# A 90 degree rotation of a matrix: hardware loops on three engines, one queue for loads and stores, all outputs gathered by row tile in pairs

## The chip, the core and the metric

## The reference

```python
def setup_inputs():
    return {
        "x": np.random.randn(8192, 8192).astype(np.float32),
        "k": 1,
    }

def reference(x: np.ndarray, k: int) -> np.ndarray:
    return np.rot90(x, k)
```

With k = 1, `out[i, j] = x[j, 8191 - i]`: a transpose whose rows then stand in reverse order. Nothing is calculated. 268 MB are read and 268 MB are written.

## The kernel before

The matrix is cut into 16 macro tiles of 1024 rows (R) and 4096 columns (W). A macro tile is loaded as T = 8 slabs of 128 rows, each slab one DMA of 2 MB (128 partitions with 16 KB each), and gives J = 8 outputs, each 512 rows of the result by 1024 columns, also one DMA of 2 MB. So there are 128 loads and 128 stores. A slab holds one block of 128 rows by 512 columns (CH) for each of the eight outputs; an output needs that block of all eight slabs, 32 squares of 128 x 128.

On-chip, a macro tile lies in a grid of 8 x 8 blocks. One macro tile lies in it by slab and output, the next one the other way round (`kk % 2`), so that a slab of the next macro tile can be placed where an output of this one has just been read. Five blocks of the grid (CORNER) lie in PSUM instead, and the places of four of these in SBUF (STAGES) serve as staging space.

Four engines work as a pipeline:

- SP (line 141) issues the loads into three landing buffers at the start and two of them later on. A load waits until the slab that last lay in its buffer has been placed (`s_copy`).
- VectorE does two things. `place` (line 156) copies a landed slab into the grid: one copy of 4096 columns, or two where part of the slab belongs in PSUM. `to_stage` (line 166) gathers half of the work of 128 x 1024 that PE takes at a time into a staging block, 512 columns, and reverses the columns within it. For each output VectorE makes eight such gathers, then places one slab of the next macro tile, `place(n - 1 + T)`. For the first output of a macro tile (`first`) the last slab is gathered straight from its landing buffer and placed after that.
- PE (line 223) transposes a staging block as four squares into one of three PSUM banks, in a hardware loop of 12 blocks.
- ACT (line 260) copies each bank, 512 columns, into an output buffer. After eight of them it drains, waits for itself (`s_act`) and issues the store (line 267) on its own DMA queue. Three output buffers take turns; for the last eight outputs five buffers do, the two landing buffers among them. For an output's first use of a buffer, ACT waits for the store that last read it (`s_store`).

The first output of a macro tile is gathered by row tile: one block of the grid gives one staging block, and ACT's copy writes four strips of 128 columns, one for each of the four row groups of the output. The other seven are gathered by column group: a staging block takes 128 columns from each of four slabs.

All streams but PE's are written out without loops: some 1350 copies on VectorE, 1024 on ACT.

The names that matter further on: `place`, `first`, `to_stage`, `pieces` (which finds the parts of a row or column of the grid, in SBUF and in PSUM), `out_buf` and `load_buf` (which buffer an output or a load takes).

## Time and profile before

| What | Value |
|---|---|
| Time, median of 3 runs | 1282.06 us (1279.53 to 1283.26) |
| The profiled execution: time | 1278.41 us |
| The profiled execution: span from first to last instruction | 1276.6 us |
| Mean granted TensorE clock | 0.771 of full |
| PE, VectorE, ACT busy | 57%, 59%, 45% of the span |
| Bytes over the span | 537.09 MB, 421 GB/s |
| One landing copy of 4096 columns (VectorE, line 156) | 2294 ns, 88 times |
| One gather of 512 columns from the grid (VectorE, line 166) | 423 ns |
| One copy out of PSUM (ACT, line 260) | 590 ns in the mean, 1024 times |
| A load from issue to landing, a store from issue to landing (median) | 17.3 us, 23.5 us |

Rows of busy time add up what one engine does; they overlap each other. The groups of instructions also give the idle time ahead of each instruction and what ended it: VectorE waits 299.2 us ahead of its landing copies, ended by a load, ACT waits 616.5 us ahead of its copies, ended by PE, and 77.9 us ended by a store that had to leave an output buffer. The share of busy DMA engines is a mean over all sixteen; the GB/s beside it are what they moved.

### The profile page before, as it was taken

The page shows a single profiled execution, that of the slowest core. Times are in us where ns is not written, and L with a number is a line of the kernel's source. Part 1 is how long each engine was busy: PE and PEld are TensorE (multiplying, and loading weights), DVE is VectorE, ACT ScalarE, POOL GpSimd, SP SyncE. Part 2 cuts the span into 40 slices and gives each one's busy share as a digit, 9 for nine tenths or more (in the row PEclk, how much of TensorE's full clock was granted, in tenths as well). Part 3 has the DMA queues.
Part 4 walks back from the last instruction along what each step waited for, and adds up shares of the span by engine and source line. Part 5 has one row for each costly group of instructions (what it writes and reads, how often), then busy time and mean ns, then how long its engine had stood idle before and what let it go on. Part 6 is the DMA issues. An engine that isn't in the chain of part 4 may idle for free. (4 is left out here: it accounts for less than half of the span.)

```text
span 1276.6 us, 13910 instructions
## 1 busy us (share of the span) xinstructions
PE 727.7 (57%) x4096; PEld 665.7 (52%) x4096; DVE 752.2 (59%) x1352; ACT 570.0 (45%) x1025; POOL 0.7 (0%) x6
## 2 busy tenths in 40 slices
PE   1555655555655655556555665556556565555666
PEld 1455555555655555555544654455555555445664
DVE  4757565565555655656565565655656555565564
ACT  1444444444444444445444454444444444444456
POOL 0000000000000000000000000000000000000000
PEclk9977787777677776777788677777876777887778
DMA  9999999999999999999999999999999999999978
GB/s 397 421 429 429 430 429 428 431 429 428 430 430 428 429 431 428 429 429 428 428 431 411 427 406 429 430 418 425 406 430 428 420 429 410 430 429 411 431 304 378
DMA packets 36889, 537.09 MB, mean 421 GB/s; under 512 B 4096, under 2 KB 4096, under 8 KB 4096
## 3 DMA queue, kind: packets, MB, share of 16 engines
q1 hardware_dynamic: 18432, 268.44, 49.7%
q10 hardware_dynamic: 18432, 268.44, 49.7%
q14 instruction: 25, 0.20, 0.0%
HBM read 268.44 MB, written 268.44 MB: 421 GB/s over the span
## 5 line engine op out<-in xcount | busy, mean ns | idle before, releaser
L223 PE MATMUL ps<-ident,grid 128*128 128x128 f32 x4096 | 727.7, 353 | 539.9 <-PEq L220 536.7
L223 PEld LDWEIGHTS ps<-ident,grid 128*128 128x128 f32 x4096 | 665.7, 189 | 601.6 <-issue 592.6
L260 ACT COPY buf<-ps 128x512 f32<-128x512 f32 x1024 | 568.7, 590 | 697.2 <-PE ps L223 616.5
L156 DVE COPY grid<-buf 128x4096 f32<-128x4096 f32 (+3 forms) x128 | 282.9, 2210 | 301.9 <-DMA buf<-in_x_dram 299.2
L166 DVE COPY grid<-grid 128x512 f32<-128x512 f32 (+2 forms) x1001 | 377.1, 409 | 141.1 <-PE ps L223 136.0
L166 DVE COPY grid<-corner 128x256 f32<-128x256 f32 (+2 forms) x160 | 66.9, 418 | 0.0
L166 DVE COPY grid<-buf 128x512 f32<-128x512 f32 x23 | 9.8, 427 | 70.5 <-DMA buf<-in_x_dram 70.5
L156 DVE COPY corner<-buf 128x1024 f32<-128x1024 f32 (+2 forms) x40 | 48.8, 1220 | 0.0
L260 ACT ACT_TABLE_LOAD x1 | 1.3, 1283 | 1.0 <-SPq L58 1.0
L121 POOL TENSOR_SCALAR_AFFINE_SELECT ident<-ident 128x128 f32<-128x128 f32 x1 | 0.3, 294 | 0.2 <-POOL ident L119 0.2
L119 POOL MEMSET ident<- 128x128 f32 x1 | 0.2, 205 | 0.5 <-SPq L58 0.5
L292 POOL MEMSET const-bfloat16-1.0<- 128x1 bf16 x1 | 0.1, 102 | 0.0
L292 POOL MEMSET const-uint8-127<- 128x1 uint8 x1 | 0.1, 102 | 0.0
L292 POOL MEMSET const-float32-0.0<- 128x1 f32 x1 | 0.1, 99 | 0.2 <-issue 0.2
L292 POOL MEMSET const-float32-1.0<- 128x1 f32 x1 | 0.1, 99 | 0.0
## 6 DMA issues: line engine op xcount, KB each, us to landing
buf<-in_x_dram SPq DMA_DIRECT2D x128, 2048.0 KB, 17.3
out_dram<-buf ACTq DMA_DIRECT2D x128, 2048.0 KB, 23.5
```

The costliest lines, as they stand in the source:

```text
L119: e.memset(ident[:], 0.0).then_inc(s_id, 1)
L121: e.affine_select(out=ident[:], in_=ident[:], compare_op=mybir.AluOpType.not_equal, fill=1.0, base=0, pattern=[[-1, P]], channel_multiplier=1,
L156: i = e.tensor_copy(out=v, in_=a[:, at : at + n, :])
L166: i = e.tensor_copy(out=s.rearrange("p (n c) -> p n c", n=v.shape[1]), in_=v[:, :, ::-1],)
L223: i = e.transpose(ps[:, at : at + P], stage(q)[:, t * P : (t + 1) * P], ident[:],)
L260: e.copy(dst, src.rearrange("p (n c) -> p n c", n=H)).then_inc(s_free, 1)
L292: nc = _bacc.Bacc("TRN2", target_bir_lowering=False, num_devices=1)
```

## The change

SP issues everything: ten loads, then store 0, store 1 and load 10, store 2 and load 11, and so on, one store and one load in turn, the last nine stores at the end. A store waits on SP for `s_act`, that is, until ACT has finished that output, and the load behind it in program order waits for it too. ACT issues no DMA any more. Loads take three landing buffers for the first eight slabs only.

All outputs are gathered by row tile. VectorE gathers two blocks of 512 columns with one copy into two staging blocks (`from_grid`, `to_stage` with n = 2), so four copies for an output; the blocks from PSUM and an odd last block are separate. PE signals the start of a block (`s_begun`, after the first of its four squares), and VectorE writes a staging place when PE has begun the block after the one that lay there. PE waits for staged blocks in pairs (`s_full`). ACT's copies all write four strips of 128 columns.

VectorE runs a hardware loop over two macro tiles a turn (seven turns), ACT one over three outputs (40 turns), PE one over 12 blocks as before. Semaphores are counted down at the end of a turn (`take`, `settle`) so that each turn waits for the same values.

At the end, the last slab of the last macro tile is not placed in the grid. Each of the last eight outputs gathers its block of it straight from the landing buffer (`from_landing`). The last eight outputs take four buffers in turn, one landing buffer and the three output buffers.

ACT also makes a copy of one column to a scratch tile before its loop.

```diff
-H = T // 2
 STAGES = [a * J + b for a, b in list(CORNER)[:4]]
+NS = len(STAGES)
 BANKS = 3
-LOOP = 4 * BANKS
+OUTS = 3
+PE_LOOP = NS * BANKS
+ACT_LOOP = OUTS * T
...
         def load_buf(m):
-            return m % 3 if m <= T else (m + 1) % 2
+            return m % 3 if m < T else m % 2
+
+        spare = load_buf(n_load - 2)
 
         def out_buf(n):
             e = n - (n_out - J)
             if e < 0:
-                return 2 + (n + 1) % 3
-            free = [load_buf(n_load - 2), load_buf(n_load - 1)]
-            free += [out_buf(n_out - J - 3 + i) for i in range(3)]
-            return free[e % 5]
+                return 2 + (n + 1) % OUTS
+            return [spare, *(out_buf(n_out - J - OUTS + i) for i in range(OUTS))][e % 4]
...
             @block.sync
+                for _ in range(T + 2):
+                    load()
+                for n in range(n_out):
+                    store(n)
+                    if n and loaded < n_load:
+                        load()
...
+                def to_stage(n, srcs):
+                    nonlocal staged
+                    e.wait_ge(s_begun, staged + 1 + n)
+                    q = staged % NS
+                    step = STAGES[q + 1] - STAGES[q] if n > 1 else 1
+                    for at, k, v in srcs:
+                        e_at = STAGES[q] + at * step
+                        i = e.tensor_copy(
+                            out=strided(grid, e_at, step, k), in_=v[:, :, ::-1]
+                        )
+                    staged += n
+                    if staged % 2 == 0:
+                        i.then_inc(s_full, 1)
...
+                def from_grid(n, tiles):
+                    kk, j = divmod(n, J)
+                    t = 0
+                    while t < tiles:
+                        k = min(2, tiles - t)
+                        to_stage(k, pieces(kk, t, k, j, 1))
+                        t += k
...
+                def macro(kk):
+                    e.drain()
+                    for n in range(kk * J + 1, (kk + 1) * J):
+                        from_grid(n, T)
+                        place(n - 1 + T)
+                    n = (kk + 1) * J
+                    e.drain()
+                    from_grid(n, T - 1)
+                    from_landing(n, n + T - 1)
...
+                with e.While(lambda: e.snap(turns) > 0):
+                    for kk in range(2):
+                        macro(kk)
+                        place((kk + 2) * T - 1)
+                    settle()
+                    e.reg_sub(turns, turns, 1)
+                macro(KK - 2)
+                e.drain()
+                for n in range(n_out - J + 1, n_out):
+                    from_grid(n, T - 1)
+                    from_landing(n, n_load - 1)
...
             @block.scalar
-                    e.drain().then_inc(s_act, 1)
-                    e.wait_ge(s_act, n + 1)
-                    e.dma_start(
+                        for t in range(T):
+                            e.wait_ge(s_done, q + 1)
+                            src = ps[:, q % BANKS * CH : (q % BANKS + 1) * CH]
+                            e.copy(
+                                o[:, t], src.rearrange("p (g c) -> p g c", g=G)
+                            ).then_inc(s_bank, 1)
+                            q += 1
+                        e.drain().then_inc(s_act, 1)
+                with e.While(lambda: e.snap(turns) > 0):
+                    run(range(OUTS))
+                    take(e, s_done, ACT_LOOP)
+                    e.reg_sub(turns, turns, 1)
+                run(range(n * OUTS, n_out))
```

## The prediction

> **What bounds the kernel now.** I read the page first, then the busy time by stretches, then VectorE's timeline, then the timeline of the end.

> ```profile
> span 1276.6 us, 13910 instructions
> ...
> q1 hardware_dynamic: 18432, 268.44, 49.7%
> q10 hardware_dynamic: 18432, 268.44, 49.7%
> ```

> The page's queue rows: loads (q1) and stores (q10) together keep the 16 DMA engines busy for 99.4% of the span, while PE, VectorE and ACT are busy for 57, 59 and 45%. The kernel is bound by moving 537 MB. What is left to ask is at which pace, and where the engines pause. Busy time by stretches (the last two columns are the DMA engines' busy share and GB/s):

> ```profile
> 60.00:600.00 540.00, 315.82 (x1748) 291.95 (x1747) 320.89 (x576) 243.41 (x437) 0.00 (x0) 0.74 1.01 429
> 600.00:1220.00 620.00, 355.01 (x1997) 327.12 (x1997) 364.41 (x662) 277.52 (x499) 0.00 (x0) 0.77 1.01 423
> ...
> 674.00:677.00 3.00, 2.96 (x20) 2.70 (x18) 1.28 (x3) 2.49 (x5) 0.00 (x0) 0.75 0.99 350
> 680.00:683.00 3.00, 2.04 (x17) 1.79 (x18) 2.64 (x8) 1.42 (x3) 0.00 (x0) 1.00 0.99 311
> ```

> ```profile
> 1224.00:1226.00 2.00, 1.20 (x6) 0.86 (x5) 0.48 (x2) 1.33 (x3) 0.00 (x0) 0.74 0.14 57
> 1226.00:1228.00 2.00, 0.63 (x4) 0.40 (x4) 2.00 (x1) 0.59 (x1) 0.00 (x0) 1.00 0.12 49
> ...
> 1236.00:1238.00 2.00, 1.95 (x17) 1.45 (x16) 1.66 (x5) 1.65 (x4) 0.00 (x0) 1.00 0.00 0
> ```

> Three things stand here. The second half moves less (423 against 429 GB/s), with holes of some 3 us in which the DMA engines count as busy but move only 311 to 350. Near the end a share of 0.12 to 0.14 is two engines of sixteen: two are late, and a transfer has landed only when its last engine is done. And at 1236 nothing moves at all. So the pace is that of the late engines, and VectorE shows it, since each landing copy starts when a load has landed in full:

> ```profile
> 85.71 2.29 DVE L156 COPY grid<-buf 128x4096 f32<-128x4096 f32 x1 [3.20 <-DMA buf<-in_x_dram]
> 95.47 2.29 DVE L156 COPY grid<-buf 128x4096 f32<-128x4096 f32 x1 [2.77 <-DMA buf<-in_x_dram]
> ...
> 529.83 2.29 DVE L156 COPY grid<-buf 128x4096 f32<-128x4096 f32 x1 [2.98 <-DMA buf<-in_x_dram]
> ...
> 569.32 2.29 DVE L156 COPY grid<-buf 128x4096 f32<-128x4096 f32 x1 [3.17 <-DMA buf<-in_x_dram]
> ...
> 677.91 2.29 DVE L156 COPY grid<-buf 128x4096 f32<-128x4096 f32 x1 [1.80 <-DMA buf<-in_x_dram]
> 688.94 2.29 DVE L156 COPY grid<-buf 128x4096 f32<-128x4096 f32 x1 [5.39 <-DMA buf<-in_x_dram]
> ```

> A load and a store take 9.76 us together at first (95.47 - 85.71), 9.87 once two engines have fallen back ((569.32 - 529.83) / 4), and 11.03 at a change of macro tile in the second half. The first loads, alone, land every 4.88 us (VectorE starts at 8.28 and 13.16); a store then costs 9.87 - 4.88 = 4.99.

> A floor from these rows: the first load counts from 8.28 - 4.88 = 3.4 us; 128 pairs x 9.87 = 1263.4; from the last landing to the end of the span 1.6 (the last store is issued at 1268.31 and lands 6.7 us later by the DMA view, at 1275.0). Sum 1268.4, against 1276.6: 8.2 us are lost. From the landing at 677.91 to the last at 1225.43 there are 55 loads in 547.5 us, 9.955 each: 55 x 0.085 = 4.7 us go in the holes at macro changes. The other 3.5 us go at the end:

> ```profile
> 1225.43 0.43 DVE L166 COPY grid<-buf 128x512 f32<-128x512 f32 x1 [3.08 <-DMA buf<-in_x_dram]
> 1225.95 2.82 DVE L156 COPY grid<-buf 128x2560 f32<-128x2560 f32 x1
> ...
> 1227.37 0.56 ACTq L267 DMA_DIRECT2D out_dram<-buf  x1
> 1228.69 1.75 DVE L156 COPY corner<-buf 128x1536 f32<-128x1536 f32 x1
> 1230.47 1.43 DVE L166 COPY grid<-grid 128x512 f32<-128x512 f32 x4
> ...
> 1237.76 0.56 ACTq L267 DMA_DIRECT2D out_dram<-buf  x1
> ```

> After the last load lands, two landing copies (2.82 and 1.75 us) stand ahead of the staging of output 121, whose store is issued 10.4 us after that of output 120. Even the late engines run dry there.

> **The change, part by part.**

> *One queue, on SP.* ACT gives up 128 issues of 0.56 us and its wait; SP takes them, alternating store n with load n+9. Now the load stands behind SP's wait for output n. Take the moment t when load n+7 has landed. Behind it in the queue are store n-1, load n+8, store n, load n+9, store n+1, due to start at t, t+5.0, t+9.9, t+14.9 and t+19.7. VectorE places slab n+7 (2.3 us), then gathers output n+1; with PE at half clock eight tiles take 8 x 0.85 = 6.8 us (ACT copies start 0.85 apart near 1190), plus some 1.7 to fill and drain: store n+1 is ready at t+10.8, 8.9 us early. Store n was ready one pair before, t+0.9; load n+9 waits for the slab placed at t+2.3, 12 us early. At a macro change the placing is 2.82 + 1.75 us and store n+1 comes at about t+13.7: 6 us early. ACT needs the buffer of store n-2, landed at t-5. So waiting behind the other kind costs nothing, with 6 to 12 us of queued transfers as cover; without it, each us of delay would be a us of time. The late engines set t, so they don't run dry.

> [...]

> What a single queue does to the transfers themselves the trace doesn't show. Loads alone run at 429 to 433 GB/s (15 to 45 us), stores alone at 421, held by their issue. In between, engines change between queues nearly every packet at 429. I take 9.87 a pair; the ends are 9.76 (the early pace; 14 us less) and the holes' price at each change of kind. A 3 us hole loses 3 x (1 - 350/429) = 0.55 us, and 236 changes would make 130 us. The steady stretch is nearer by far: it has more changes, not fewer.

> *The holes.* They come when one queue has run empty on most engines and starts again beside the other: at 671 to 674 stores have 74% of the share, then a load comes in. With one queue no second one wakes up. I take them as gone (-4.7); the other end is that they stay.

> *VectorE in pairs.* Eight gathers of 427 ns per output become four; 128, 256 and 512 columns took 225, 292 and 423 ns, a line that gives some 0.70 us for 1024, so 2.8 us in place of 3.4. VectorE waits 299 us for loads before placing, so this gains nothing. From the PSUM corner the row with 1024 columns is 1.22 us, hidden likewise. A coarser wait (two tiles) adds up to 0.85 us to an output, inside the slack.

> *Loops.* PE had one before; ACT's 40 turns and VectorE's 7 are new. Branches and register operations aren't shown. If each turn had to fetch code, the price is bounded by 0 and by a start from idle: the first load is issued at 0.96 us and data flow from about 2.0, so 1 us, a few under load. The 6 to 9 us cover both; on the path I take 0. Code fetched in all is 25 packets on q14, with 85 turns of PE's loop among them, so a loop need not fetch again. [...]

> *The start.* Load 8 now waits for slab 6 (placed by 41.05 us) in place of slab 5; load 7 lands at 42.5 and an issue needs about 1 us: 0 to 0.5 us lost, I take 0.3.

> *The end.* After the last load come stores 119 to 127, 9 x 4.99 = 44.9 us. Output 120 was issued 1.94 us after that landing before; one more tile makes it 2.8, under the 5.0 of store 119. Slab 127 is no longer placed, so output 121 follows at once: 6.8 us at half clock, 4.95 at full (1242.70 to 1247.65, ACT's copies and its issue, which now leaves). In the end of before the clock rose from 0.50 to 1.00 some 5 us after PE began at 1231. I allow 0.7 us and take the rest of the 3.5 as gained. Without this cover the end costs what it costs now.

> Sum: 1268.4 + 0.3 + 0.7 = 1269.4, a span 7.2 us shorter. The profiled execution took 1278.41 in all, 1.8 over its span; the median of the runs is 1282.06. Taking 7.2 off the median gives 1274.9, so **1275**, 0.55% faster. Its own range is 1271 to 1279 (holes gone or not, the start and the end at their bounds).

> **Rivals.**

> *The late engines catch up* (12%). In the first 100 us all keep 9.76; if one queue keeps them so, 128 x 9.76 = 1249.3, with the floor's 3.4 and 1.6 and the 1.0 of start and end 1255.3, a median of 1261. Against it: nothing in the change touches what makes two engines late.

> *The holes stay* (20%). Engines that are ahead still run dry at a macro change and start again together: 1269.4 + 4.7 = 1274.1, 2.5 under the span of before, a median of 1279.6: 0.2% better, which can't be told from before. For it: only the late engines are covered by my slack. Against: no second queue.

> *Slower: a change of kind inside one queue costs* (21%). [...] It decides from (1286 - 1275) / 236 = 0.05 us a change; at 0.1 us it makes 24 us, a median of 1299, at the hole's price 1405. For it: the trace has no such change and the holes show that changes can cost. Against: the mixed 429.

> *No effect on the queue at all* (the loops alone, blocked loads giving back the end) falls into the second rival's time.

> **How the numbers follow.** The forecast has 47%, the rivals 12, 20 and 21. About 0.3% (3.8 us) is what a measurement can tell from no change: faster is under 1278.2. Of the forecast's 47, 44 lie there, of the holes' 20 some 4: faster 0.60; within 0.3% 0.19; slower 0.21. The range 1259 to 1287 takes in the catching-up case but for its lower tail, both middle cases, and the slower one only where its price is under 0.05 us.

> **What would show it.** Right: one queue with 537 MB and a busy share near 0.99, landings on VectorE every 9.87 us to the end, none of 10.5 or more at macro changes, the last landing near 1222, and stores after it without a stretch of zero. Slow-pair rival: landings at 10 us or more throughout with the share at 1.0. Wrong altogether: DMA share well under 0.99 between 60 and 1220 us, with SP waiting for ACT while loads are due; then my slack is mistaken.

## The result, and the profile after

| | before | after |
|---|---|---|
| Time, median of 20 runs each, in turn on one chip | 1279.74 us (1276.67 to 1284.07) | 1274.62 us (1270.13 to 1281.05) |
| Ratio, 95% interval | | 0.9957 (0.9942 to 0.9972) |
| The profiled execution: time, span | 1278.41, 1276.6 us | 1274.65, 1272.9 us |

The kernel became 0.4% faster. By the medians that is 5.1 us, by the two profiled executions 3.7 us. One execution of the same kernel differs from the next by more than this (the changed kernel's runs spread over 11 us), so a trace tells where time goes, and only the medians of several runs tell how much a version is worth.

The page of the changed kernel:

```profile
span 1272.9 us, 11874 instructions
...
q1 hardware_dynamic: 36864, 536.89, 99.9%
q14 instruction: 5, 0.04, 0.0%
...
L200 DVE COPY grid<-grid 128x1024 f32<-128x1024 f32 x476 | 319.8, 673 | 265.7 <-PE ps L272 262.5
L189 DVE COPY grid<-buf 128x4096 f32<-128x4096 f32 (+1 forms) x127 | 279.8, 2203 | 213.9 <-DMA buf<-in_x_dram 213.9
```

One queue now carries both halves at the busy share that two had (99.9%, before 49.7% on each of two). The row of gathers mixes two shapes: 441 gathers of two blocks, 692 ns each (0.70 us was assumed), and 35 of one block, 426 ns each. VectorE still waits 213.9 us for loads: it isn't the bound.

Busy time by stretches, first one of the kernel before, then those of the changed kernel; the last two columns are the DMA engines' busy share and GB/s:

```profile
40.00:60.00 20.00, 12.14 (x77) 10.61 (x78) 16.36 (x27) 9.25 (x17) 0.00 (x0) 1.00 1.00 414
```

```profile
40.00:60.00 20.00, 12.48 (x72) 11.08 (x72) 14.14 (x15) 9.96 (x18) 0.00 (x0) 1.00 0.99 373
60.00:600.00 540.00, 318.88 (x1737) 296.43 (x1738) 296.94 (x303) 242.11 (x433) 0.00 (x0) 0.72 1.01 428
600.00:1220.00 620.00, 360.05 (x2010) 332.19 (x2009) 340.62 (x348) 280.39 (x503) 0.00 (x0) 0.76 1.01 423
772.00:776.00 4.00, 2.89 (x14) 2.92 (x15) 2.35 (x4) 1.23 (x3) 0.00 (x0) 0.54 1.02 365
...
1233.00:1239.00 6.00, 5.35 (x41) 4.44 (x42) 3.54 (x6) 5.45 (x12) 0.00 (x0) 1.00 1.02 427
```

Between 60 and 1220 us the kernel moves 428 and 423 GB/s, as before (429 and 423): nothing is won there, and the holes are still there (365 GB/s at a share of 1.02). Between 40 and 60 us it moves 373 where the kernel before moved 414: 20 x (414 - 373) / 429 = 1.9 us lost. At the end, where the kernel before had a stretch of zero at 1236, this one moves 427.

VectorE's timeline, each landing copy starting when a load has landed in full, the end, and SP's issues of stores 120 and 121:

```profile
100.42 2.29 DVE L189 COPY grid<-buf 128x4096 f32<-128x4096 f32 x1 [2.11 <-DMA buf<-in_x_dram]
...
543.34 2.30 DVE L189 COPY grid<-buf 128x4096 f32<-128x4096 f32 x1 [3.12 <-DMA buf<-in_x_dram]
...
572.78 2.29 DVE L189 COPY grid<-buf 128x4096 f32<-128x4096 f32 x1 [1.63 <-DMA buf<-in_x_dram]
...
681.40 2.29 DVE L189 COPY grid<-buf 128x4096 f32<-128x4096 f32 x1 [1.09 <-DMA buf<-in_x_dram]
...
1225.80 0.43 DVE L200 COPY grid<-buf 128x512 f32<-128x512 f32 x1 [2.50 <-DMA buf<-in_x_dram]
...
1231.30 0.43 DVE L200 COPY grid<-buf 128x512 f32<-128x512 f32 x1 [0.22 <-PE ps L272]
...
1235.82 0.43 DVE L200 COPY grid<-buf 128x512 f32<-128x512 f32 x1 [0.22 <-PE ps L272]
```

```profile
1228.99 0.55 SPq L158 DMA_DIRECT2D out_dram<-buf  x1
...
1233.68 0.54 SPq L158 DMA_DIRECT2D out_dram<-buf  x1
```

The quiet pace is (572.78 - 543.34) / 3 = 9.81 us a pair, a little better than the 9.87 of two queues. But over the second half, from the load at 681.40 (at 677.91 before) to the last at 1225.80, 55 loads take 544.4 us, 9.90 each: 544.4 - 55 x 9.81 = 4.8 us still go in holes. The last load lands 0.37 us later than before (1225.43). From there to the end of the span it is 1272.9 - 1225.80 = 47.1 us, against 1276.6 - 1225.43 = 51.2: 4.1 us, which is the whole gain of this execution. The copies at 1231.30 and 1235.82 show why: the last slab's blocks for outputs 121 and 122 go straight from the landing buffer, 4.5 us apart, with no placing between.

### The profile page after: what moved, and what is told of

It is laid out like the page before. It is cut to its first block, busy times and chain, and to the rows that moved or that the text cites. A ratio compares the mean times of both kernels' runs of the same rounds, so it can differ in the third digit from the quotient of the medians.

```text
span 1272.9 us, 11874 instructions
## 1 busy us (share of the span) xinstructions
PE 732.8 (58%) x4096; PEld 674.8 (53%) x4096; DVE 692.8 (54%) x719; ACT 571.4 (45%) x1026; POOL 0.7 (0%) x6
## 2 busy tenths in 40 slices
DMA packets 36869, 536.93 MB, mean 422 GB/s; under 512 B 4096, under 2 KB 4096, under 8 KB 4096
## 3 DMA queue, kind: packets, MB, share of 16 engines
q1 hardware_dynamic: 36864, 536.89, 99.9%
HBM read 268.44 MB, written 268.44 MB: 422 GB/s over the span
## 5 line engine op out<-in xcount | busy, mean ns | idle before, releaser
L272 PEld LDWEIGHTS ps<-ident,grid 128*128 128x128 f32 x4096 | 674.8, 191 | 585.4 <-issue 535.8
L200 DVE COPY grid<-grid 128x1024 f32<-128x1024 f32 x476 | 319.8, 673 | 265.7 <-PE ps L272 262.5
L189 DVE COPY grid<-buf 128x4096 f32<-128x4096 f32 (+1 forms) x127 | 279.8, 2203 | 213.9 <-DMA buf<-in_x_dram 213.9
L200 DVE COPY grid<-corner 128x1024 f32<-128x1024 f32 (+1 forms) x47 | 48.4, 1029 | 23.8 <-PE ps L272 23.8
L200 DVE COPY grid<-buf 128x512 f32<-128x512 f32 x30 | 12.8, 427 | 63.0 <-DMA buf<-in_x_dram 61.8
L317 ACT ACT_TABLE_LOAD x1 | 1.3, 1283 | 1.1 <-SPq L62 1.1
## 6 DMA issues: line engine op xcount, KB each, us to landing
buf<-in_x_dram SPq DMA_DIRECT2D x128, 2048.0 KB, 17.3
```

The lines of the kernel that those rows point to most:

```text
L189: i = e.tensor_copy(out=v, in_=a[:, at : at + n, :])
L200: i = e.tensor_copy(out=strided(grid, e_at, step, k), in_=v[:, :, ::-1])
L272: i = e.transpose(ps[:, at : at + P], strided(grid, STAGES[q % NS], 1, 1)[:, 0, g * P : (g + 1) * P], ident[:],)
L317: e.copy(scratch[:], ident[:, :1])
```

## The experiments

Each ratio is against the kernel before, run in turn with it on the same chip, with its 95% interval. The runs lay on four chips: the loops, two queues, one queue alone and the slab placed on one; the changed kernel again, the end alone, single blocks and the third buffer on the next; earlier and later stores on a third; lighter gathers on a fourth.

### The parts one by one

*The loops.* VectorE's and ACT's loops written out; the rest as changed.

```diff
-                with e.While(lambda: e.snap(turns) > 0):
-                    for kk in range(2):
-                        macro(kk)
-                        place((kk + 2) * T - 1)
-                    settle()
...
+                for kk in range(KK - 2):
+                    macro(kk)
+                    place((kk + 2) * T - 1)
+                    if kk % 2:
+                        settle()
...
-                with e.While(lambda: e.snap(turns) > 0):
-                    run(range(OUTS))
+                for turn in range(n):
+                    run(range(turn * OUTS, (turn + 1) * OUTS))
```

> The changed kernel with VectorE's and ACT's hardware loops written out again (PE's loop stays, as in both kernels). If loops cost nothing on the path, as I forecast: 0.996 of before, within 0.2% of the changed kernel, and the 25 or so packets of code are back. If the loops' turns cost time, this is faster than 0.994.

Measured: 1275.71 us, 0.9979 (0.9966 to 0.9993), a span of 1272.5. Without the loops it isn't faster. Code fetched (q14) is 18 packets here against 5 with the loops, so the 47 turns of the two loops didn't each fetch their code again. The difference in time lies within the intervals; single packets come back further down, under the macro changes.

*Two queues again.* The changed kernel with the stores issued by ACT on its own queue (ACT's loop written out).

```diff
@block.sync
-                for _ in range(T + 2):
+                for _ in range(n_load):
                     load()
-                for n in range(n_out):
-                    store(n)
-                    if n and loaded < n_load:
-                        load()
...
@block.scalar
...
                         e.drain().then_inc(s_act, 1)
+                        store(n)
```

> The changed kernel with the stores issued by ACT on its own queue again (ACT's loop written out for it). Theory A, the joined queue brings the gain: the landings' period in quiet stretches goes back from 9.80 to 9.86 us, the stores' lag of two DMA engines to some 12 us, and the time to 0.999 of before. Theory B, the gain lies in the end of the kernel and the joined queue only costs at the start: the 2 to 3 us lost between 40 and 60 us come back and the time is 0.993 of before.

Measured: 1276.93 us (1272.36 to 1282.92), 0.9991 (0.9973 to 1.0009). VectorE's timeline and two stretches of this kernel:

```profile
530.69 2.29 DVE L170 COPY grid<-buf 128x4096 f32<-128x4096 f32 x1 [2.40 <-DMA buf<-in_x_dram]
...
570.12 2.29 DVE L170 COPY grid<-buf 128x4096 f32<-128x4096 f32 x1 [1.70 <-DMA buf<-in_x_dram]
```

```profile
40.00:60.00 20.00, 11.44 (x72) 9.83 (x72) 13.47 (x14) 9.79 (x18) 0.00 (x0) 1.00 0.99 390
...
600.00:1220.00 620.00, 365.71 (x2011) 338.77 (x2011) 341.12 (x350) 281.80 (x504) 0.00 (x0) 0.73 1.01 425
```

The quiet pace goes back to (570.12 - 530.69) / 4 = 9.86. So the 9.81 is the single queue's. Between 40 and 60 us this kernel moves 390 GB/s in place of 373. What that is worth in the end isn't settled: this interval overlaps that of the written-out loops on the same chip, and the profiled execution, with a span of 1270.5, is the fastest of its twelve runs, so its trace mustn't be held against the changed kernel's.

*One queue alone.* The kernel before, with SP issuing loads and stores in the order of the change, ACT only signalling.

```diff
@block.sync
+                for m in range(T + 2):
+                    load(m)
+                for n in range(n_out):
...
+                    e.wait_ge(s_act, n + 1)
...
+                    e.dma_start(out=..., in_=...).then_inc(s_store[b], 16)
...
+                    if n and n + T + 1 < n_load:
+                        load(n + T + 1)
...
@block.scalar
-                    e.wait_ge(s_act, n + 1)
...
-                    e.dma_start(...)
```

> The kernel before, with SP issuing its stores too, in the changed kernel's order; nothing else. Theory A: period 9.80, 0.997 of before. Theory B: the first change from loads to stores in the queue costs 2 us near 50 us, the end runs dry as before, and the time is 1.000 to 1.002 of before.

Measured: 1281.69 us, 1.0022 (1.0013 to 1.0031): 2.8 us slower. Stretches of this kernel:

```profile
60.00:600.00 540.00, 309.48 (x1728) 285.82 (x1726) 317.50 (x572) 239.98 (x433) 0.00 (x0) 0.75 1.01 427
600.00:1220.00 620.00, 366.17 (x2012) 339.96 (x2010) 364.32 (x661) 281.60 (x504) 0.00 (x0) 0.74 1.01 422
1222.00:1240.00 18.00, 11.17 (x62) 10.36 (x63) 11.54 (x21) 7.91 (x15) 0.00 (x0) 0.72 0.61 257
```

A single queue by itself doesn't gain: 427 and 422 GB/s are a little under the 429 and 423 of two, and the end still runs dry. In the changed kernel, by the run above, one queue and two can't be told apart by the time.

*The end.* Once taken out of the changed kernel (the last slab placed in the grid), once put alone into the kernel before (its last eight outputs gathering their block of slab 127 from the landing buffer, with four output buffers in turn).

```diff
+                place(n_load - 1)
...
                 for n in range(n_out - J + 1, n_out):
-                    from_grid(n, T - 1)
-                    from_landing(n, n_load - 1)
+                    from_grid(n, T)
```

> The changed kernel, but slab 127 is placed in the grid and the last seven outputs gather from there. Theory B (the end): two copies of 2.3 us or more stand ahead of output 121 again, the DMA engines run dry for 4 to 5 us, and the time is 0.999 to 1.000 of before. Theory A (the queue): at most 2 us are lost, 0.997.

> The kernel before with the changed end alone: slab 127 stays in its landing buffer, the last seven outputs gather their part of it from there, and the last eight take four buffers. If the end is the gain, as the loss of 0.4% without it says: 0.996 to 0.997 of before, and no stretch without bytes near 1236 us. If it only pays together with the joined queue, whose late engines lag less: 0.999 or more.

Measured: taken out 1279.18 us, 0.9998 (0.9987 to 1.0009), so nothing of the gain is left; put in alone 1276.74 us, 0.9986 (0.9975 to 0.9997). VectorE and SP at the end of the kernel with the slab placed:

```profile
1222.78 0.43 DVE L200 COPY grid<-buf 128x512 f32<-128x512 f32 x1 [2.49 <-DMA buf<-in_x_dram]
1223.13 2.81 DVE L189 COPY grid<-buf 128x2560 f32<-128x2560 f32 x1
1225.86 1.75 DVE L189 COPY corner<-buf 128x1536 f32<-128x1536 f32 x1
1225.98 10.00 SPq L158 DMA_DIRECT2D out_dram<-buf  x2
```

The two landing copies are back ahead of output 121, and its store goes out at 1225.98 + 10.00 - 0.55 = 1235.43, 9.4 us after that of output 120 (4.7 us in the changed kernel). The end is the part whose worth is shown in both directions: 0.14% alone, and without it the change brings nothing that can be measured. (The changed kernel itself has no run on the chip of the first of these two; the kernel with loops written out has one, at 0.9979, and its interval just overlaps this one's.) The parts do not add up: 0.14% for the end, a loss of 0.22% for the queue alone, and 0.34 to 0.43% for all together. Gathering all outputs by row tile, and PE's earlier signal, were not run by themselves, so what they add isn't known.

*Pairs.* Each block gathered by a copy of its own, eight an output.

```diff
-                        k = min(2, tiles - t)
+                        k = 1
```

> The changed kernel with one block per gather in place of pairs: 8 copies of 427 ns an output. If VectorE's time is covered by the waits for loads, as I forecast: the same as the changed kernel, 0.996. If the pairs carry the gain: 0.998 or more.

> The changed kernel as it is, beside the others on this chip: 0.9957 of before, between 0.994 and 0.997.

Measured: singles 1275.89 us, 0.9978 (0.9969 to 0.9987); the changed kernel again, on the same chip, 1274.83 us, 0.9966 (0.9953 to 0.9979). The intervals overlap: the pairs save VectorE 49 us (917 gathers of single blocks took 369.0 us; the same blocks in 441 pairs and 35 single ones 319.8), and these are under cover.

### The start

Load 8 in the third landing buffer, as the kernel before has it, and load 9 in the next (VectorE's loop written out for it).

```diff
-            return m % 3 if m < T else m % 2
+            return m % 3 if m <= T else (m + 1) % 2
```

> The changed kernel with load 8 in the third landing buffer and load 9 in the next one, as before had them (VectorE's loop is written out for it). If the 2 to 3 us lost between 40 and 60 us come from loads 8 and 9 being issued late: they are back (the 20 us from 40 to 60 move 415 GB/s or more, not 373) and the time is 0.994 of before. If they come from the queue's first change from loads to stores: no change, 0.996.

Measured: 1274.88 us, 0.9966 (0.9953 to 0.9979), the same as the changed kernel beside it. Its stretches (this execution was the slowest of its five):

```profile
40.00:60.00 20.00, 12.02 (x72) 10.55 (x72) 14.13 (x15) 9.87 (x18) 0.00 (x0) 1.00 1.01 419
60.00:600.00 540.00, 316.62 (x1731) 293.56 (x1732) 296.43 (x303) 241.89 (x432) 0.00 (x0) 0.73 1.01 426
600.00:1220.00 620.00, 363.60 (x2011) 337.31 (x2010) 337.74 (x346) 280.78 (x502) 0.00 (x0) 0.74 1.00 420
```

The start is back at 419 GB/s, so the loss there is the buffer's and not that of the queue's first turn from loads to stores (one queue alone, with three buffers, ran at 419 there too). Yet the time is the same: what the start gains went in the holes, 426 and 420 GB/s in place of 428 and 423. As this was the slowest of its executions, the size of that is uncertain.

What is lost at the start can also be read from load 10, on VectorE, in the changed kernel and in the one with the third buffer:

```profile
70.62 2.29 DVE L189 COPY grid<-buf 128x4096 f32<-128x4096 f32 x1 [6.42 <-DMA buf<-in_x_dram]
```

```profile
67.96 2.29 DVE L189 COPY grid<-buf 128x4096 f32<-128x4096 f32 x1 [4.02 <-DMA buf<-in_x_dram]
```

It lands 2.7 us later without the third buffer. SP issues load 8 at 40.94 in place of 35.70 and load 9 at 45.82 in place of 40.86: both come some 5 us later, since load 8 waits for slab 6 in place of slab 5 and load 9 for slab 7 in place of slab 6.

### The macro changes

In the changed kernel's end one sees how far most DMA engines run ahead of the last one. Stretches of it again:

```profile
1225.00:1226.00 1.00, 0.00 (x0) 0.00 (x0) 0.20 (x1) 0.00 (x0) 0.00 (x0) 1.00 0.66 279
...
1227.00:1228.00 1.00, 1.00 (x7) 1.00 (x6) 0.55 (x1) 0.51 (x1) 0.00 (x0) 0.50 0.31 131
1228.00:1229.00 1.00, 1.00 (x7) 1.00 (x6) 0.44 (x1) 0.67 (x2) 0.00 (x0) 0.50 0.08 33
```

Behind the last load, landed in full at 1225.80, the queue holds store 119 and nothing else until store 120 is issued at 1228.99. The last engine takes 5.03 us for it, from 1225.77 (its update of the last load) to 1230.80. But the share falls from 1225 on: other engines have finished store 119 already, some 5 us ahead of the last one. A store issued 6.7 us before the last engine needs it is then only some 1.7 us early for the leading ones. Four runs tried whether this makes the holes: the store made earlier (with two and with three landing buffers), made later, and VectorE's work made lighter.

*Earlier.* PE waits for single blocks, and the last slab of a macro tile is placed in the middle of the next one's first gathers (VectorE's loop written out for it).

```diff
...
+                    steps = place_steps(kk * T + T - 1)
+                    from_grid(n, 4)
+                    next(steps)
+                    from_grid(n, 6, 4)
+                    for _ in steps:
+                        pass
...
+                    from_grid(n, T, 6)
+                    place(n - 1 + T)
...
-                        if q % 2 == 0:
-                            e.wait_ge(s_full, q // 2 + 1)
+                        e.wait_ge(s_full, q + 1)
```

> The changed kernel with two things moved at a macro change: PE waits for each gathered block instead of each pair, so the macro tile's first output is ready about 0.85 us (a gather and its wait) sooner, and the last slab of a macro tile is placed in the middle of the next macro tile's first output's gathers instead of before them, so that the store after it is issued about 2 us sooner (the two grid copies of a slab and their wait are 2.2 us) and the load into the freed buffer about as much later. Theory A (the extra time at macro changes comes from stores issued too late for the DMA engines that run ahead in the one queue): the late changes go, 600 to 1220 us runs at 427 to 429 GB/s instead of 423, landings of 10.4 us and more at macro changes are mostly gone, and the time is 0.990 to 0.993 of before, 4 to 8 us below the changed kernel. Theory B (the macro change itself, its addresses or the copy to the grid, stretches the transfers whatever the issue): 0.996, 423 GB/s as in the changed kernel. Theory C (the later load is what is missed then): slower than the changed kernel, 0.998 to 1.002.

> The kernel of early_stores with loads 8 and 9 in the landing buffers that they have in the kernel before (VectorE's loop written out for it). Theory A: no late stores, and the 2 us at the start come back too: 0.988 to 0.991. Theory B: the 2 us at the start are given back in the macro changes as in the run with the third buffer alone: 0.996 to 0.998.

Measured: 1277.02 us, 0.9981 (0.9970 to 0.9993); with the third buffer 1274.83 us, 0.9958 (0.9943 to 0.9973). Neither gains the 4 to 8 us. Stretches and SP's timeline of the first:

```profile
40.00:60.00 20.00, 10.44 (x68) 8.67 (x68) 14.35 (x15) 9.28 (x17) 0.00 (x0) 1.00 0.88 324
...
600.00:900.00 300.00, 174.39 (x976) 159.47 (x976) 164.50 (x168) 136.74 (x244) 0.00 (x0) 0.77 1.01 427
900.00:1220.00 320.00, 187.90 (x1024) 173.14 (x1024) 175.95 (x181) 143.58 (x256) 0.00 (x0) 0.74 1.01 423
```

```profile
1069.18 0.54 SPq L158 DMA_DIRECT2D out_dram<-buf  x1
1074.99 0.33 SPq L149 DMA_DIRECT2D buf<-in_x_dram  x1
1078.59 0.55 SPq L158 DMA_DIRECT2D out_dram<-buf  x1
```

From 600 to 900 us the holes shrink (427 against 423 in the changed kernel), after 900 they don't: now it is the load that comes late, 5.8 us after the store ahead of it, since its buffer is freed later. (By the times of the single engines, used below, that load was issued 0.9 us before the leading engine needed it, and took that engine 6.1 us.) At the start the same delay costs (324 GB/s between 40 and 60 us, 2.3 us more than in the changed kernel); the third buffer takes that back (0.9981 to 0.9958). The third of the expected ways, that the later load is missed, is what happened.

*Later.* The grid copied onto itself once at each macro change.

```diff
+                    e.drain()
+                    e.tensor_copy(out=grid[:, : J * CH], in_=grid[:, : J * CH])
                     e.drain()
                     for n in range(kk * J + 1, (kk + 1) * J):
```

> The changed kernel with an extra copy of the grid's 4096 columns onto itself on VectorE at each macro change, where the second store of a macro tile waits for it: that store is about 2.3 us later (4 copies of 128x1024 take 2.7 us by the trace, so between 2 and 3). The output is not touched. Theory A: nearly every macro change now starves the DMA engines that run ahead, in the first half too; 60 to 600 us drops from 428 to about 424 GB/s, and the time is 5 to 12 us above the changed kernel, 1.000 to 1.006 of before. Theory B: 0.996 to 0.997, as the changed kernel, since the late engines still have some 6 us of slack.

Measured: 1281.12 us, 1.0022 (1.0010 to 1.0033).

*Lighter.* A gather from the grid copies a quarter of its columns, and PE waits for single blocks.

```diff
-                            out=strided(grid, e_at, step, k), in_=v[:, :, ::-1]
+                            out=strided(grid, e_at, step, k)[:, :, :cols],
+                            in_=v[:, :, ::-1][:, :, :cols],
...
-                        to_stage(k, pieces(kk, t, k, j, 1))
+                        to_stage(k, pieces(kk, t, k, j, 1), CH // 4)
...
```

> The changed kernel in which a gather from the grid copies only the first 128 of a block's 512 columns (the other columns of the staging slots keep older data, so most of the output is not the rotation), and PE waits for each gather by blocks instead of by pairs. DMA work, order and placing are unchanged; VectorE is some 1.7 us an output lighter (four gathers of 0.67 us to about 0.25), so the store after the first of a macro tile comes about 3 us sooner and no load comes later. Theory A (stores and loads issued less than some 3 us ahead of the leading DMA engines are what stretches transfers): 600 to 1220 us runs at 427 to 429 GB/s, landings of 10.4 us and more are gone after 60 us, time 0.990 to 0.993 of before. Theory B (the leading DMA engines run on until they meet the issue whatever its lead, or the macro change stretches transfers by itself): 423 to 424 GB/s and 0.995 to 0.997, as the changed kernel. A cover that is only partly enough would lie between.

Measured: 1272.29 us, 0.9951 (0.9938 to 0.9963). The same macro change in three kernels, SP issuing a store and a load, VectorE placing the load ahead of them and then that load. The changed kernel, the one with later stores, the one with lighter gathers:

```profile
763.42 0.54 SPq L158 DMA_DIRECT2D out_dram<-buf  x1
764.00 0.59 SPq L149 DMA_DIRECT2D buf<-in_x_dram  x1
...
770.07 2.29 DVE L189 COPY grid<-buf 128x4096 f32<-128x4096 f32 x1 [3.02 <-DMA buf<-in_x_dram]
...
781.18 2.29 DVE L189 COPY grid<-buf 128x4096 f32<-128x4096 f32 x1 [3.48 <-DMA buf<-in_x_dram]
```

```profile
767.24 0.54 SPq L158 DMA_DIRECT2D out_dram<-buf  x1
767.82 0.59 SPq L149 DMA_DIRECT2D buf<-in_x_dram  x1
771.85 2.29 DVE L189 COPY grid<-buf 128x4096 f32<-128x4096 f32 x1 [0.69 <-DMA buf<-in_x_dram]
...
783.22 2.29 DVE L189 COPY grid<-buf 128x4096 f32<-128x4096 f32 x1 [4.26 <-DMA buf<-in_x_dram]
```

```profile
760.88 0.54 SPq L158 DMA_DIRECT2D out_dram<-buf  x1
761.46 0.59 SPq L149 DMA_DIRECT2D buf<-in_x_dram  x1
...
768.20 2.29 DVE L189 COPY grid<-buf 128x4096 f32<-128x4096 f32 x1 [4.81 <-DMA buf<-in_x_dram]
778.26 2.29 DVE L189 COPY grid<-buf 128x4096 f32<-128x4096 f32 x1 [3.16 <-DMA buf<-in_x_dram]
```

| | store issued ahead of the landing before it | from that landing to the next |
|---|---|---|
| later stores | 771.85 - 767.24 = 4.6 us | 11.37 us |
| changed kernel | 770.07 - 763.42 = 6.7 us | 11.11 us |
| lighter gathers | 768.20 - 760.88 = 7.3 us | 10.06 us |

The GB/s of 40 equal slices of the span (some 32 us each) show the same over the whole run: changed kernel, later stores, lighter gathers.

```profile
GB/s 395 395 424 425 430 429 429 430 429 429 429 427 430 429 426 427 424 429 427 419 429 417 428 429 412 430 410 428 430 421 430 417 429 424 418 430 411 430 380 381
```

```profile
GB/s 396 392 427 428 412 428 426 427 430 412 429 430 427 428 413 430 430 429 429 416 427 430 430 426 400 428 420 432 424 396 429 425 430 423 385 429 421 427 391 378
```

```profile
GB/s 397 395 427 426 429 428 429 427 430 430 429 429 430 429 429 429 430 430 429 421 429 429 430 430 416 430 427 430 429 419 428 426 429 422 417 429 418 427 390 365
```

With later stores the dips come in the first half too (412, 412, 413) and are deeper in the second (400, 396, 385); with lighter gathers the first half has none, and the second fewer. The mean of slices 4 to 38 is 423.0, 425.5 and 427.1 GB/s in the order later, changed, lighter. By the time, the later stores are told apart from the changed kernel: 15 copies of 2.29 us on an engine that is 54% busy cost 7 to 8 us (1.0022 against 0.9957 and 0.9966), some 0.5 us at each macro change. The lighter gathers are not: 0.9951 lies inside the changed kernel's interval, and dips are left (416, 419, 417).

*Engine by engine.* The traces keep one thing more. For each transfer they hold the times of sixteen updates of its semaphore (4096 for the 256 transfers of the changed kernel). The updates carry no engine's name; they are read here as one from each of the sixteen DMA engines. For store 119 of the changed kernel nine engines end 4.5 to 4.8 us ahead of the last one, five 2.4 to 2.6 us and one 1.7 us. Call the first of the sixteen times that of the leading engine. The cover of a store for the leading engine is then the time from the store's issue on SP to that engine's end of the transfer ahead. The table takes all 1264 stores issued between 60 and 1200 us in the eleven traces with one queue (the changed kernel twice, its variants but two queues, and one queue alone); times are medians in us, from the first of the sixteen times of one transfer to the first of the next (leading), or from last to last.

| cover for the leading engine | stores | the store, leading engine | the store, last engine | the load behind it, leading and last |
|---|---|---|---|---|
| 3 us and more | 1125 | 4.90 | 4.93 | 4.86, 4.86 |
| 2.5 to 3 | 50 | 4.91 | 4.94 | 4.98, 4.87 |
| 2 to 2.5 | 31 | 5.06 | 4.94 | 5.22, 5.27 |
| 1.5 to 2 | 36 | 5.41 | 4.96 | 5.38, 4.97 |
| 1 to 1.5 | 13 | 5.74 | 4.93 | 5.71, 5.48 |
| 0.5 to 1 | 3 | 6.26 | 4.90 | 5.75, 5.67 |
| under 0.5 | 6 | 6.73 | 4.99 | 5.91, 6.24 |

What the leading engine lacks of some 2 us of cover it loses on the store (6.73 us under 0.5 us of cover, in place of 4.90); the last engine loses nothing there (4.90 to 4.99). But the load behind the store then takes longer on the last engine too, not every time, but by up to 1.4 us in the median, and that is what VectorE's landings show. The macro change by itself does nothing of the kind: at the first four in this stretch of the changed kernel the stores had 3 us or more (stores 8 to 33, the first two of each macro tile), and the leading engine took 4.89 to 4.97 us for them.

Over the changed kernel the lead of the first engine over the last grows from 3.2 us at store 8 to 5.7 us at store 112. The first store of a macro tile is issued 6.6 to 8.2 us before the last engine needs it all along; for the leading engine that falls from 3.1 to 4.1 us at the first four macro changes to 1.3 us at store 112. Six stores have under 2 us: 56, 64, 80, 104 and 112, the first ones of their macro tiles, and 73, a second one. The changed kernel run again has four such stores, the one with lighter gathers three, with later stores seven, with the third buffer ten. Of the 4.8 us lost over the changed kernel's last 55 loads, 3.9 fall on loads right behind a store with under 3 us of cover.

Another 0.7 us fall on load 104, which is late on the last engine alone (5.58 us; 4.85 on the leading one). A packet of code is fetched at 995.7 us, within that load's time on the last engine (993.1 to 998.7). The only other packet of code between 75 and 1220 us, at 363.7, falls within load 40's (360.6 to 366.2), which is 0.7 us late in the same way. In the kernel before with one queue, which fetches 23 packets in this stretch, twelve stores are late by 0.7 to 1.0 us on the last engine alone, with a packet in the time of each. So not all that looks like a hole is late issue. That the packets of code cause these delays is argued from their times alone.

So late issue makes most of the holes of the changed kernel (3.9 of the 4.8 us). With more cover the leading engine was also further ahead: with lighter gathers 6.3 us at store 104 (5.8 in the changed kernel), and about half of the holes in the second half stayed.

What stays open: why the load behind a late store takes longer on all engines, the last one too; why some engines lag at all; and why two queues have runs from 1272 to 1283 us. No run could take away the lead of the leading engines, so the holes without it weren't tried.

## Why the prediction came out

**The time.** 1275.0 was forecast and 1274.62 measured, but the size of the gain was not as close as that: 7.2 us were expected, 5.1 came by the medians and 3.7 in the profiled executions. The median of three runs from which the 7.2 were taken, 1282.06, lies 2.3 us over the median of twenty, 1279.74; that filled the gap, by luck: 7.2 us off the median of twenty would have been 1272.5. The span forecast, 1269.4, compares with 1272.9, and all of that miss lies ahead of the last landing (1269.4 - 47.2 = 1222.2 against 1225.80).

**The end was right,** in its mechanism and its size, but for one term. After the last landing 44.9 + 0.7 + 1.6 = 47.2 us were forecast and 47.1 came. The store of output 121 is 4.7 us behind that of 120 instead of 10.4, and the stretch of zero is gone. Store 120 came 3.2 us after the last landing (2.8 were forecast), so the leading engines stood still for a while (share 0.08 at 1228). The 0.7 us were allowed for output 121 at half clock. But the clock was back at 1.00 from 1230 us on, and most of the loss came at store 120, which took the last engine 5.5 us: the size of this term fits, its place doesn't. The runs with this part alone and without it bear it out: 0.14% and the whole gain.

**The holes were wrong.** The step that failed reads "With one queue no second one wakes up. I take them as gone (-4.7)". The holes stayed: 4.8 us over the last 55 loads by landings against a quiet pace of 9.81. Behind it lies the step on SP's queue, "store n+1 comes at about t+13.7: 6 us early" and "The late engines set t, so they don't run dry." The cover was worked out well (6.7 us at the macro change shown, 17.3 - 4.87 = 12.4 us for a load), but for the late engines alone. The leading one is 5.1 to 5.8 us ahead at the six late stores; 1.3 to 2 us are left for it, and a hole there lengthened the next load on the last engine too behind four of the six (5.1 to 6.2 us in place of 4.86). The step also looked at the second store of a macro tile only; five of the six are first stores. The rival "the holes stay" gave this very reason, and its mechanism held beside the end's gain; its time, a median of 1279.6, left the pace at 9.87.

**The pace was slightly mis-sized.** 9.87 a pair was taken from two queues; one queue runs at 9.81 in its quiet stretches. A little of the rival "the late engines catch up" is in it: 0.06 x 128 = 7.7 us at most, given back in the holes and at the start, so that 60 to 1220 us moves nearly the same bytes as before. They did not catch up: the last engine is still 4.8 us behind the first at store 119.

**The start was mis-sized.** 0.3 us was the price of load 8 alone; the stretch from 40 to 60 us lost 1.9 us, and load 10 landed 2.7 us later than with the third buffer. The step left out load 9, which waits one slab longer too. That the loss comes with the missing third buffer is shown by the 419 GB/s.

**The slower rival was wrong.** A turn from loads to stores inside one queue has no price that the quiet pace shows: with two turns a pair, 9.81 is under 9.86 and 9.87. One queue alone cost 2.8 us in the kernel before, which over 236 turns would be 0.01 us each; the forecast's point of decision was 0.05.

**Loops and pairs at nothing:** held by the times. Neither made a difference that the intervals tell from none. The row that the prediction read as one from the PSUM corner, 1.22 us, is a copy into it; copies of 1024 columns out of it took 1.23 us in the changed kernel, hidden as forecast.

**What would show it.** One queue with 537 MB at 0.999: came. Landings every 9.87 to the end with none of 10.5 or more at macro changes, and the last near 1222: didn't come (11.11 at 781.18; 1225.80). Stores without a stretch of zero: came.

## What to carry to other kernels

Here cover had to be counted for the engines that run ahead and not only for those that set the landing: the six late stores, queued some 7 us ahead of the slowest DMA engine, were 1.3 to 2 us ahead of the fastest, and that was too little (5.3 to 5.8 us on it in place of 4.9); here some 2.5 us were enough for a store (4.91). Though this kernel is bound by DMA, work on a compute engine was worth taking out of a place where it stands ahead of a store: the last tile, which need not be placed in the grid first (0.14% by itself). And before one kernel's trace is held against another's for a few us, look at the spread of the runs: a gain taken off a median of three runs was here off by 2.3 us.

## What the runs showed of the hardware

- In one queue, alternating 2 MB loads and stores ran at 9.81 us a pair; in two, at 9.86 to 9.87. Joining them alone made the kernel before 0.22% slower all the same.
- 15 copies of 2.29 us on VectorE, which had 580 us of idle time, cost 7 to 8 us. Each delayed one store; six of these had under 2 us of cover for the leading DMA engine, and the load behind each of the six took 1.1 to 1.7 us longer on the last engine.
- A store with 2.5 us or more of cover for the leading engine took it 4.9 us, with under 0.5 us of it 6.7 us; the last engine took 4.9 to 5.0 us either way.
- The changed kernel's streams of loops fetched 5 packets of code, written out 18, and the kernel before 25. Single packets came with a delay of 0.7 to 1.0 us of one transfer on the last engine; over a whole run no difference in time could be told from it.
